# Local attention's transposes and weighted values two steps behind its scores

## The chip, the cores and the metric
The kernel runs on one NeuronCore of one Trainium2 chip. The metric is the device time of one execution in microseconds (us); the median of three runs stands for a kernel. Engines go by their short names: PE (TensorE), DVE (VectorE), ACT (ScalarE), POOL (GpSimd), SP (SyncE, which only issues DMAs).

## The reference
A decoder trunk of two layers over 1024 tokens of width 1024. Each layer normalizes x, projects it with one matrix `w_in`, and feeds three mixers side by side; their gated results go through `w_out` and are added to x.

```python
h = rms_norm(x, norm_g); proj = h @ w_in                # split into the parts below
y_mla  = mla_mixer(q_lat, kv_lat, k_rope, ...) * silu(g_mla)   # latent attention, causal
y_conv = short_conv_mixer(c_h, c_b, c_c, conv_w) * silu(g_conv)
y_swa  = swa_mixer(s_q, s_k, s_v, ...) * silu(g_swa)    # local attention, window 128
x = x + concat([y_mla, y_conv, y_swa]) @ w_out
```

The change is in `swa_mixer`: 8 query heads in two groups (`kv` 0 and 1) of four heads that share keys and values; queries and keys normalized per head; a block of 128 queries sees its own 128 keys and the 128 before; scores get a distance penalty, a softmax with one extra "sink" logit, and then weight the values.

## The kernel before
Products are made as three fp32r matmuls of high and low parts (`mm3`, lines 188 to 190). Each layer has three phases. **Phase 1** (pool `p1`) makes all local attention, and beside it the projections of the latents and a part of the gates. **Phase 2** (pool `cp`) makes the rest of the projection and the convolution; its `u` tiles are in a pool `uc` of their own on the right side of the memory. **Phase 3** makes the output projection and the latent attention.

Phase 1 is a software pipeline written out by hand. Its list `steps` has 17 entries: (kv 0, block 0 to 7), an empty one, (kv 1, block 0 to 7). A step goes through four functions:

- `swa_a` (a): projects 320 columns (24 matmuls), ACT squares, DVE sums, POOL takes the inverse root, DVE writes the normalized `qn` (line 316).
- `swa_b` (b): PE transposes `qn` (L326, L329), ACT and DVE write high and low parts of keys and queries `sx` (L333 to L337); PE makes the scores in `ps_s` (L350, 8 matmuls); DVE adds the penalty and takes maxima (L354, four, each followed by a short read of its maximum); ACT takes exponentials into a tile `pr` (L359) and DVE the reciprocals of the sums; POOL scales `pr` (L365, four heads). `ps_s` has one buffer, `pr` two.
- `swa_d` (d): PE transposes the scaled `pr` (L375, 8), ACT and DVE write their high and low parts `sy` (L376, L377, two each).
- `swa_e` (e): PE multiplies by the values (L385, 4 matmuls), ACT moves half of it (L389, L390), DVE adds into `osw` (L393, two).

The order within one iteration i is `'badfe'`: b of step i-1, a of step i, d of step i-2, then `f`, then e of step i-2. `f` runs as many "units" as the list `P1_FILL` says for that iteration: eight `unit_b` and eight `unit_a` (latents and values, 24 matmuls of 256 or 288 columns), then gate units `unit_m` (24 matmuls of 512 columns, an ACT copy L410 and a store L412). When certain units are done, `fill` asks for the weights of later ones (`after`): four loads on SP (L149) into three raw tiles, casts (L171) and subtractions (L173). Gate weights 0 are asked for behind the sixteenth unit and gate weights 1 behind the twentieth; the units right behind these use them.

The program text gives priorities; the order of instructions on each engine is laid down when the kernel is built, by a planned time. On the chip each engine then takes its instructions in that order, and a waiting instruction holds what stands behind it.

Of the kernel before, what the change touches and what calls it, by code (L numbers as in the profile page):

```python
# [10 lines left out]
F32 = mybir.dt.float32  # L11
# [8 lines left out]
P = 128  # L20
# [26 lines left out]

X_BEFORE, X_ALONE, X_FREE = 1, 7, 2
P1_ORDER = 'badfe'
P1_FILL = ([0, 0, 2, 1, 0, 1, 1, 2, 1, 2, 0, 0, 2, 1, 0, 1, 0, 2, 0, 1],  # L50
           [2, 2, 2, 2, 0, 0, 2, 1, 1, 1, 1, 1, 0, 1, 1, 1, 1, 1, 1, 1])
C1_STEP = 3
O_STARTS = [0, 0, 0, 0, 0, 0, 0, 0, 0, 0, 0, 0, 0, 1, 0, 0, 0, 0, 2, 0, 2, 1, 2, 1, 1, 1, 3, 2, 0, 0, 0, 0]
O_LIGHT = [0, 0, 0, 0, 0, 0, 0, 0, 0, 0, 0, 0, 0, 0, 0, 0, 0, 0, 0, 0, 0, 0, 0, 0, 0, 0, 0, 0, 1, 1, 0, 2]
# [9 lines left out]
def f32(ap):  # L64
    return ap.bitcast(F32)
# [3 lines left out]
def trunk(ctx, tc, x, norm_g, w_in, w_qb, w_kvb, w_out, c_gain, c_rope, c_idb, c_ali, out):  # L69
# [4 lines left out]
    def phase_pool(name, bufs=1):  # L74
        cm = tc.tile_pool(name=name, bufs=bufs, reuse_waits="tile")
        return cm, cm.__enter__()
# [23 lines left out]
    def ps_s():  # L100
        return pp["pool"].tile([P, 1024], F32, name="ps_s", tag="S", bufs=pp["n"][0])

    def ps_t():
        return pp["pool"].tile([P, 512], F32, name="ps_t", tag="T", bufs=pp["n"][1])
# [140 lines left out]
    for l in range(depth):  # L245
# [45 lines left out]
        def load_c(kv):  # L291
            return load_w([win[:, :, O_SQ + kv * 256:O_SQ + kv * 256 + 256],
                           win[:, :, O_SK + kv * 64:O_SK + kv * 64 + 64]], 8, eng=(v, g) if kv == 1 else g)

        uc_cm = tc.tile_pool(name=f"uc{l}", bufs=2, reuse_waits="tile", side="right")
        uc = uc_cm.__enter__()
        p1_cm, p1 = phase_pool(f"p1{l}")
        ali = p1.tile([P, H, 2 * P], BF16, name="ali")
        if l:
# [8 lines left out]
        def swa_a(kv, t, w):  # L308
            o = group_mm(t, w, WMAX)
            qn = p1.tile([P, 5, 2, 64], F32, name="qn", tag="qn", bufs=2)  # L310
            sq = qn.rearrange("p h o d -> p (h o d)")[:, 0:WMAX]
            s.activation(out=sq, in_=o, func=AF.Square)
            ss = small.tile([P, 5], F32, name="sss")
            v.tensor_reduce(out=ss, in_=sq.rearrange("p (h d) -> p h d", h=5), axis=AX.X, op=ALU.add)
            r = rsqrt("sr", ss, 5, 1.0 / 64, EPS)
            v.tensor_tensor(
                out=qn,
                in0=o.rearrange("p (h o d) -> p h o d", h=5, o=1).broadcast_to([P, 5, 2, 64]),
                in1=r.rearrange("p (h o u) -> p h o u", o=1, u=1).broadcast_to([P, 5, 2, 64]),
                op=ALU.mult)  # L320
            wq[kv, t] = qn.rearrange("p h o d -> p (h o d)")

        def swa_b(kv, t):
            qf = wq.pop((kv, t))
            tk = ps_t()
            pe.transpose(tk[:, 0:P], qf[:, 4 * P:5 * P], idn)  # L326
            tq = ps_t()
            for h in range(4):
                pe.transpose(tq[:, h * P:(h + 1) * P], qf[:, h * P:(h + 1) * P], idn)  # L329
            qs = qst[:, t % 2]  # L330
            kh = kst[:, 0, (t + 1) * P:(t + 2) * P]
            kl = kst[:, 1, (t + 1) * P:(t + 2) * P]
            s.mul(kh, tk[:, 0:P], skg[:, l:l + 1])  # L333
            v.scalar_tensor_tensor(out=kl, in0=tk[:, 0:P], scalar=skg[:, l:l + 1],
                                   in1=f32(kh), op0=ALU.mult, op1=ALU.subtract)
            s.mul(qs, tq, sqg[:, l:l + 1])
            v.scalar_tensor_tensor(out=qs[64:128], in0=tq[64:128], scalar=sqg[64:128, l:l + 1],  # L337
                                   in1=f32(qs[64:128]), op0=ALU.mult, op1=ALU.subtract)
            sc = ps_s()
            m = small.tile([P, 4], F32, name="sm")  # L340
            nm = small.tile([P, 4], F32, name="snm")
            ls = small.tile([P, 4], F32, name="sls")
            es = small.tile([P, 4], F32, name="ses")
            ri = small.tile([P, 4], F32, name="sri")
            pr = p1.tile([P, 4, 256], F32, name="pr", tag="pr", bufs=2)
            k0 = 0 if t else P
            sk4 = snk[:, l, kv * 4:kv * 4 + 4]
            for h in range(4):
                for a in range(2):
                    pe.matmul(sc[:, h * 256:(h + 1) * 256], lhsT=qs[:, h * P:(h + 1) * P],  # L350
                              rhs=kst[:, a, t * P:(t + 2) * P], start=(a == 0), stop=(a == 1))
            for h in range(4):
                so = sc[:, h * 256:(h + 1) * 256]
                v.tensor_tensor_reduce(out=so[:, k0:], in0=so[:, k0:], in1=ali[:, kv * 4 + h, k0:], scale=1.0,  # L354
                                       scalar=sk4[:, h:h + 1], op0=ALU.add, op1=ALU.max, accum_out=m[:, h:h + 1])
            v.tensor_scalar(out=nm, in0=m, scalar1=-1.0, scalar2=None, op0=ALU.mult)
            v.tensor_tensor(out=es, in0=sk4, in1=m, op=ALU.subtract)
            for h in range(4):
                s.activation(out=pr[:, h, k0:], in_=sc[:, h * 256 + k0:(h + 1) * 256], func=AF.Exp,  # L359
                             bias=nm[:, h:h + 1], scale=1.0, accum_out=ls[:, h:h + 1])  # L360
            marks["exp"] = s.activation(out=es, in_=es, func=AF.Exp)
            v.tensor_tensor(out=ls, in0=ls, in1=es, op=ALU.add)
            v.reciprocal(out=ri, in_=ls)  # L363
            for h in range(4):
                g.tensor_scalar(out=pr[:, h, k0:], in0=pr[:, h, k0:], scalar1=ri[:, h:h + 1], scalar2=1.0,  # L365
                                op0=ALU.mult, op1=ALU.mult)
            wprob[kv, t] = pr

        def swa_d(kv, t):
            pr = wprob.pop((kv, t))  # L370
            blks = (0, 1) if t else (1,)
            for blk in blks:
                tp = ps_t()
                for h in range(4):
                    pe.transpose(tp[:, h * P:(h + 1) * P], pr[:, h, blk * P:(blk + 1) * P], idn)  # L375
                s.copy(out=pts[:, blk, 0], in_=tp)  # L376
                v.tensor_tensor(out=pts[:, blk, 1], in0=tp, in1=f32(pts[:, blk, 0]), op=ALU.subtract)  # L377
# [68 lines left out]
        steps = [(0, t) for t in range(NT)] + [None] + [(1, t) for t in range(NT)]  # L446

        def fetch(key, parts, **how):
            W[key] = load_w(parts, 8, **how)
# [13 lines left out]
        def fill(n=1):  # L463
            for _ in range(n):
                k = n_done[0]
                if k == len(units):
                    return
                if k >= 2 * NT and k % 4 == 0:
                    W["gate"] = W[k // 4 - NT // 2, "g"]
                units[k]()  # L470
                n_done[0] += 1
                if k in after:
                    key, parts = after[k]
                    if key == "a":
                        fetch(key, parts)
                    else:
                        fetch((key, "g"), parts, **({"eng": v, "cast": s.copy} if key > 1 else {}))
                if k == 2 * NT - 1:
                    nc.sync.dma_start(out=lat_d, in_=latf[:, :NT * 416])

        nf = P1_FILL[min(l, 1)]
        if l == 0:
# [2 lines left out]
                if k >= X_FREE:  # L485
                    fill(1)
        fill(nf[0])
        for i in range(len(steps) + 2):
            cur, prv, old = (steps[k] if 0 <= k < len(steps) else None for k in (i, i - 1, i - 2))
            for op in P1_ORDER:  # L490
                if op == "b" and prv:
                    swa_b(*prv)
                if op == "a" and cur:
                    swa_a(*cur, W[cur[0]])
                if op == "d" and old:
                    swa_d(*old)
                if op == "e" and old:
                    swa_e(*old)
                if op == "f":
                    if i == C1_STEP:  # L500
                        W[1] = load_c(1)
                    fill(nf[i + 1])
            if pending and i:
                pending.pop(0)()
        close(p1_cm)

        cp_cm, cp = phase_pool(f"cp{l}")

        def st():
# [707 lines left out]
```

## Time and profile before

| | us |
|---|---|
| median of three runs | 1569.14 |
| lowest and highest of them | 1568.62, 1573.13 |
| the profiled execution, its whole time | 1572.78 |
| its span, first to last instruction | 1571.0 |
| PE busy in the span | 1488.8 |

The profile is one execution. Each engine's instructions have a start and a duration; where an engine sat idle, the profile names what ended the idle time. The granted clock says at which share of full speed PE ran: 1.00 is 2.4 GHz and 0.50 is 1.2 GHz. Phase 1 of the first layer lies at about 50 to 246 us, that of the second at about 810 to 1026 us.

### The profile page before, as it was taken

The numbers are of one execution on the slowest core, as the hardware profiler recorded it, in microseconds if no ns is written. First come the engines' busy times: TensorE is split into PE (matmuls) and PEld (weight loads), VectorE is DVE, ScalarE is ACT, GpSimd is POOL, SyncE is SP. The second block draws the span as 40 slices with busy tenths as digits, with TensorE's granted clock in tenths as the row PEclk, the third lists the DMA queues.
The fourth block names the chain that finished last, engine by engine and source line by source line (L and its number), as shares of the span: only waits on it lengthen the run. The fifth ranks groups of instructions, "written<-read, shape, count | busy, mean of one in ns | idle before, by whom it ended". The sixth has DMA issues, their size and how long they took to land.

```text
span 1571.0 us, 25506 instructions
## 1 busy us (share of the span) xinstructions
PE 1488.8 (95%) x9084; PEld 1317.0 (84%) x9084; DVE 1104.3 (70%) x2197; ACT 721.6 (46%) x1755; POOL 737.6 (47%) x960
## 2 busy tenths in 40 slices
PE   6899989999999999999989898999999999999998
PEld 5898878788879988888788897778888899888887
DVE  6666676867685668887657755668677756788964
ACT  4354454423321258976524444443232212788851
POOL 6434431544435646874244433324444456568640
PEclk9999999999999999999999999999999999999999
DMA  6101221133356510013241102221332663100123
GB/s 206 34 1 29 85 74 54 34 94 94 101 185 183 182 48 1 8 56 107 81 130 34 29 1 85 74 55 45 103 94 87 210 209 124 48 1 15 48 75 134
DMA packets 119521, 127.98 MB, mean 81 GB/s; under 512 B 16737, under 2 KB 102625, under 8 KB 118626
## 3 DMA queue, kind: packets, MB, share of 16 engines
q1 hardware_dynamic: 119394, 126.35, 25.6%
q8 instruction: 72, 1.18, 0.3%
q14 instruction: 55, 0.45, 0.1%
HBM read 95.65 MB, written 30.67 MB: 80 GB/s over the span
## 4 chain that ended last, share of the span: by engine, by line
PE 75%; DVE 8%; ACT 7%; issue 4%; POOL 3%; DMA 2%; SPq 0%; POOLq 0%; ACTq 0%; DVEq 0%
PE ps_g L188 13%; PE ps_g L190 13%; PE ps_g L189 13%; PE ps_b L604 8%; PE ps_a L604 6%; PE ps_c L604 5%; PE ps_s L943 4%; PE ps_g L987 4%; DMA wraw<-in_w_in_dram 2%; PE ps_s L350 2%; ACT apr L956 2%; PE ps_g L385 2%; PE ps_t L973 1%; PE ps_t L375 1%; POOL wlo L173 1%
## 5 line engine op out<-in xcount | busy, mean ns | idle before, releaser
L173 POOL TENSOR_TENSOR wlo<-wraw,whi 128x512 fp32r<-128x512 f32 (+2 forms) x120 | 165.9, 1391 | 130.2 <-DVE whi L171 102.1
L188 PE MATMUL ps_g<-whi,xh 128*128 128x320 f32 (+2 forms) x512 | 158.6, 310 | 5.9 <-ACT pr L359 1.8
L190 PE MATMUL ps_g<-whi,xl 128*128 128x320 f32 (+2 forms) x512 | 156.9, 306 | 0.0
L189 PE MATMUL ps_g<-wlo,xh 128*128 128x320 f32 (+2 forms) x512 | 156.8, 306 | 0.0
L190 PE MATMUL ps_g<-whi,yl 128*128 128x256 f32 x512 | 148.1, 289 | 5.5 <-DVE yl L694 5.5
L188 PE MATMUL ps_g<-whi,yh 128*128 128x256 f32 x512 | 149.1, 291 | 0.5
L189 PE MATMUL ps_g<-wlo,yh 128*128 128x256 f32 x512 | 147.1, 287 | 0.0
L987 PE MATMUL ps_g<-pt,vs 128*128 128x256 f32 (+1 forms) x640 | 121.1, 301 | 13.7 <-DVE pt L982 8.5
L365 POOL TENSOR_SCALAR pr<-pr,sri 128x256 f32<-128x256 f32 (+1 forms) x128 | 59.2, 482 | 124.5 <-DVE sri L363 90.5
L987 PEld LDWEIGHTS ps_g<-pt,vs 128*128 128x128 f32 x640 | 91.9, 191 | 25.2 <-DVE pt L982 14.8
L982 DVE TENSOR_TENSOR pt<-ps_t,pt 128x512 fp32r<-128x512 f32 (+1 forms) x160 | 100.2, 632 | 17.3 <-ACT pt L981 15.0
L943 PE MATMUL ps_s<-kt,qh 96*128 96x512 f32 (+3 forms) x384 | 106.9, 363 | 1.0 <-ACT apr L956 0.3
L171 DVE CAST whi<-wraw 128x512 fp32r<-128x512 f32 (+2 forms) x128 | 79.6, 631 | 39.7 <-PE ps_b L604 15.9
L959 POOL TENSOR_SCALAR apr<-apr,ari 128x896 f32<-128x896 f32 (+2 forms) x80 | 72.0, 900 | 74.1 <-DVE ari L958 63.0
L190 PEld LDWEIGHTS ps_g<-whi,yl 128*128 128x128 f32 x512 | 100.3, 196 | 6.9 <-DVE yl L694 6.9
L188 PEld LDWEIGHTS ps_g<-whi,xh 128*128 128x128 f32 x512 | 99.8, 195 | 7.6 <-issue 2.8
L981 ACT CAST pt<-ps_t 128x512 fp32r<-128x512 f32 (+1 forms) x160 | 85.7, 543 | 36.1 <-PE ps_g L190 17.6
L947 DVE TENSOR_REDUCE am<-ps_s 128x1 f32<-128x128 f32 (+7 forms) x128 | 95.6, 750 | 9.3 <-PE ps_s L945 7.0
L188 PEld LDWEIGHTS ps_g<-whi,yh 128*128 128x128 f32 x512 | 100.5, 196 | 1.8 <-DVE xr L745 0.9
L189 PEld LDWEIGHTS ps_g<-wlo,xh 128*128 128x128 f32 x512 | 99.7, 195 | 1.4
L188 PE MATMUL ps_g<-xh,whi 128*128 128x512 f32 x256 | 100.7, 393 | 0.0
L189 PE MATMUL ps_g<-xl,whi 128*128 128x512 f32 x256 | 100.5, 393 | 0.0
(252 smaller groups left out, 4487.6 us busy)
## 6 DMA issues: line engine op xcount, KB each, us to landing
wraw<-in_w_in_dram SPq DMA_DIRECT2D x104, 256.0 KB, 2.9
wraw<-in_w_out_dram SPq DMA_DIRECT2D x80, 256.0 KB, 3.0
x1p<-xr SPq DMA_DIRECT2D x16, 512.0 KB, 3.3
p<-x1p SPq DMA_DIRECT2D x16, 512.0 KB, 3.6
x<-in_x_dram SPq DMA_DIRECT2D x8, 512.0 KB, 4.9
gm_d<-st SPq DMA_DIRECT2D x16, 256.0 KB, 2.0
a<-in_w_in_dram SPq DMA_DIRECT2D x16, 256.0 KB, 3.3
xr<-in_x_dram SPq DMA_DIRECT2D x8, 512.0 KB, 5.3
```

What stands on the lines that cost most here:

```text
L171: cast(out=hi, in_=raw)
L173: e.tensor_tensor(out=lo, in0=raw, in1=f32(hi), op=ALU.subtract)
L188: pe.matmul(o, lhsT=lh, rhs=rh, start=(i == 0), stop=False)
L189: pe.matmul(o, lhsT=lh, rhs=rl, start=False, stop=False)
L190: r = pe.matmul(o, lhsT=ll, rhs=rh, start=False, stop=(i == n - 1))
L604: pe.matmul(o, lhsT=a[:, k], rhs=b[:, k], start=(first and k == 0 and i == 0), stop=(k == 3 and i == 2), skip_group_check=True)
L943: pe.matmul(sp[:, kk], lhsT=a[:, hs], rhs=kt[0:QK, b, h, kk], start=(ai == 0), stop=(ai == 2 and c0 + w < n))
L947: v.tensor_reduce(out=m, in_=sp[:, :n], axis=AX.X, op=ALU.max)
L959: g.tensor_scalar(out=pr[:, :n], in0=pr[:, :n], scalar1=ri, scalar2=1.0, op0=ALU.mult, op1=ALU.mult)
L981: s.copy(out=pt[:, 0, lo_c:], in_=tp[:, lo_c:])
L982: v.tensor_tensor(out=pt[:, 1, lo_c:], in0=tp[:, lo_c:], in1=f32(pt[:, 0, lo_c:]), op=ALU.subtract)
L987: pe.matmul(av[:, q0:], lhsT=vb, rhs=pt[:, a, q * 256 + q0:(q + 1) * 256], start=(bb == 0 and bi == 0 and a == 0), stop=(last and bi == 1 ...
```

## The change
Functions d and e take step i-3 where they took step i-2, so the loop runs 20 iterations, not 19. A third buffer holds the one more `pr` that is alive. The pool `uc` is opened behind phase 1 instead of ahead of it. The units are spread anew: each layer still runs as many of them inside phase 1.

```diff
-P1_FILL = ([0, 0, 2, 1, 0, 1, 1, 2, 1, 2, 0, 0, 2, 1, 0, 1, 0, 2, 0, 1],
-           [2, 2, 2, 2, 0, 0, 2, 1, 1, 1, 1, 1, 0, 1, 1, 1, 1, 1, 1, 1])
+P1_FILL = ([0, 0, 2, 1, 0, 1, 1, 2, 1, 1, 1, 0, 1, 1, 1, 1, 0, 1, 0, 1, 1],
+           [2, 2, 2, 2, 0, 0, 2, 1, 1, 1, 1, 0, 1, 0, 1, 1, 1, 1, 1, 1, 1])
-        uc_cm = tc.tile_pool(name=f"uc{l}", bufs=2, reuse_waits="tile", side="right")
-        uc = uc_cm.__enter__()
         p1_cm, p1 = phase_pool(f"p1{l}")
-            pr = p1.tile([P, 4, 256], F32, name="pr", tag="pr", bufs=2)
+            pr = p1.tile([P, 4, 256], F32, name="pr", tag="pr", bufs=3)
-        for i in range(len(steps) + 2):
-            cur, prv, old = (steps[k] if 0 <= k < len(steps) else None for k in (i, i - 1, i - 2))
+        for i in range(len(steps) + 3):
+            cur, prv, old = (steps[k] if 0 <= k < len(steps) else None for k in (i, i - 1, i - 3))
-                    fill(nf[i + 1])
+                    fill(nf[i + 1] if i + 1 < len(nf) else 0)
         close(p1_cm)
+        uc_cm = tc.tile_pool(name=f"uc{l}", bufs=2, reuse_waits="tile", side="right")
+        uc = uc_cm.__enter__()
         cp_cm, cp = phase_pool(f"cp{l}")
```

The first entry of each list runs ahead of the loop; entry i+1 belongs to iteration i.

## Rows read from the trace of the kernel before
**Rows 1.** The page's busy times: engine, busy us, share, instructions.
```profile
PE 1488.8 (95%) x9084; PEld 1317.0 (84%) x9084; DVE 1104.3 (70%) x2197; ACT 721.6 (46%) x1755; POOL 737.6 (47%) x960
```
**Rows 2.** Windows: stretch, length, busy us per engine, PE clock, DMA; phase 1 twice.
```profile
50.00:246.00 196.00, 178.54 (x1132) 162.33 (x1131) 129.87 (x352) 90.96 (x293) 78.94 (x130) 0.97 0.15 46
810.00:1026.00 216.00, 200.24 (x1289) 183.26 (x1288) 137.78 (x364) 95.77 (x311) 87.19 (x144) 0.96 0.15 45
```
**Rows 3.** PE's waits, 40 to 260 us: us in total, times, longest.
```profile
PE ps_t L375 <- POOL pr L365: 6.6, 3, 3.8
PE ps_g L385 <- ACT sy L376: 3.5, 7, 0.6
PE ps_s L350 <- DVE sx L337: 3.4, 1, 3.4
PE ps_s L350 <- ACT pr L359: 2.4, 1, 2.4
```
**Rows 4.** PE's waits, 800 to 1040 us.
```profile
PE ps_g L385 <- ACT sy L376: 4.7, 6, 1.6
PE ps_t L375 <- POOL pr L365: 2.3, 2, 1.9
PE ps_s L350 <- DVE sx L337: 2.2, 4, 1.0
...
PE ps_s L350 <- ACT pr L359: 1.8, 1, 1.8
```
**Rows 5.** PE in order of time, first layer's end: start, us, instruction, idle before it.
```profile
205.03 0.44 PE L375 MATMUL ps_t<-idn,pr 128*128 128x128 f32 x2 [1.70 <-POOL pr L365]
...
213.14 0.39 PE L189 MATMUL ps_g<-xl,whi 128*128 128x512 f32 x1
213.37 0.39 PE L190 MATMUL ps_g<-xh,wlo 128*128 128x512 f32 x1
...
219.06 1.20 PE L350 MATMUL ps_s<-sx 128*128 128x256 f32 x8
...
231.28 2.06 PE L375 MATMUL ps_t<-idn,pr 128*128 128x128 f32 x8 [3.82 <-POOL pr L365]
233.29 2.07 PE L350 MATMUL ps_s<-sx 128*128 128x256 f32 x8
```
**Rows 6.** Windows of 5 us where PE's clock fell, both layers.
```profile
230.00:235.00 5.00, 3.73 (x16) 2.87 (x17) 3.38 (x8) 3.40 (x9) 1.85 (x4) 0.60 0.14 52
235.00:240.00 5.00, 5.00 (x18) 4.05 (x18) 2.56 (x11) 1.98 (x9) 0.00 (x0) 0.72 0.01 3
895.00:900.00 5.00, 2.20 (x11) 1.91 (x12) 3.89 (x13) 1.35 (x7) 4.41 (x7) 0.66 0.25 59
900.00:905.00 5.00, 4.28 (x19) 3.77 (x18) 3.32 (x10) 3.93 (x14) 3.03 (x7) 0.50 0.12 41
905.00:910.00 5.00, 5.00 (x33) 4.79 (x33) 0.74 (x3) 0.82 (x3) 0.02 (x1) 0.82 0.01 3
```
**Rows 7.** DVE in order of time, from 223 us.
```profile
223.09 0.69 DVE L173 TENSOR_TENSOR wlo<-wraw,whi 128x512 fp32r<-128x512 f32 x1 [1.41 <-ACT whi L171]
...
224.70 0.49 DVE L354 CUSTOM_DVE_ANT_0 ps_s<-ps_s,ali,gains 128x256 f32<-128x256 f32 x1
...
232.49 0.75 DVE L337 SCALAR_TENSOR_TENSOR sx<-ps_t,gains,sx 64x512 fp32r<-64x512 f32 x1
```
**Rows 8.** ACT and POOL in the same stretch.
```profile
228.13 0.47 ACT L359 ACTIVATE pr<-ps_s,snm 128x256 f32<-128x256 f32 x1 [3.10 <-DVE ses L357]
...
230.74 1.85 POOL L365 TENSOR_SCALAR pr<-pr,sri 128x256 f32<-128x256 f32 x4 [9.92 <-ACT gt L410]
```
**Rows 9.** PE's scores of two neighbouring steps, each beside one unit.
```profile
88.78 1.11 PE L350 MATMUL ps_s<-sx 128*128 128x256 f32 x8
...
99.48 1.20 PE L350 MATMUL ps_s<-sx 128*128 128x256 f32 x8
```
**Rows 10.** Waits of SP's queue, 200 to 270 us.
```profile
SPq L412 <- ACT gt L410: 15.2, 2, 12.6
```

## The prediction
> **What bounds the kernel now.** I read the page's busy times first: PE is busy for 1488.8 of 1571.0 us and nobody else is near it [rows 1]. So an edit that adds and removes no instruction, as this one, can only win PE's idle time and the time in which PE ran at the lower clock. The windows come second, to see how much of both lies where the edit acts. In phase 1 PE is idle for 196.0 - 178.5 = 17.5 us of the first layer and 216.0 - 200.2 = 15.8 us of the second, and the mean clock is 0.97 and 0.96 [rows 2]; elsewhere in the span the edit touches nothing. Third, PE's waits in these two stretches say who ends the idle time. Four causes carry most of it: the transposes wait for the scaled probabilities from POOL (6.6 + 2.3 us), the weighted values wait for the eviction of those transposes (3.5 + 4.7 us), the scores wait for the keys and queries (3.4 + 2.2 us), and the scores wait for the exponentials of the step before, which hold the one score tile (2.4 + 1.8 us) [rows 3, 4]. The edit speaks to the first directly, to the second in part, to the other two not at all.
>
> Fourth, one such wait in order of time. At 227.5 us PE has run dry; the transposes start at 231.28 behind 3.82 us of idle time, the scores of the following step only at 233.29 [rows 5]. The reason lies up the chain: DVE stands in front of a weight subtraction that came late (1.41 us for ACT's cast), so the penalty of these scores starts at 224.70, though they were begun at 219.06 [rows 5, 7]; ACT's exponentials then start at 228.13 and POOL scales from 230.74 [rows 8]. After this gap the clock is at 0.60 and 0.72 in the next two windows [rows 6]: PE works at 1.2 GHz for a while.
>
> **The change, part by part.**
>
> *Transposes and values one iteration later.* Each of 16 steps per layer keeps its 8 (first block of a group: 4) transposes, its ACT casts, DVE subtractions, 4 (or 2) value matmuls, copies and adds; they move behind one more projection, one more score step and one more unit group. POOL's scaling (1.85 us for four heads, rows 8) isn't moved, so nothing on POOL's queue changes place. On ACT and DVE the moved evictions now stand beside the exponentials of a step two younger; per iteration their number is the same. What they give: the tile that the transposes read was scaled a whole iteration ago, so their wait goes: 6.6 + 2.3 = 8.9 us [rows 3, 4].
>
> *The clock.* In the first layer the lower clock after 231 us lasts 2 x (0.40 x 5 + 0.28 x 5) = 6.8 us, nearly all of it busy; work done at half speed there costs 3.3 us more than at full speed [rows 6]. It follows the longest of the removed waits, so I count it: 3.3. In the second layer the windows from 895 give 2 x (0.34 + 0.50 + 0.18) x 5 = 10.2 us at half speed, of which about 8.3 busy, a cost of 4.1 [rows 6]. That fall has a wait of 1.8 us for the exponentials in front of it, which stays, beside one of 1.9 us for the probabilities, which goes [rows 4]. I count half: 2.0.
>
> *Values behind their eviction.* Where an iteration has no unit, nothing stands between transposes and values, and PE waits up to 0.6 us (first layer) or 1.6 us (second) [rows 3, 4]. The moved step doesn't help by itself. The new spread does: iterations without a unit fall from six to four in the first layer (from three to four in the second), and both loops now end with a unit in each of the last two iterations. I count 3.0 of the 8.2 us; the bounds are nothing and 8.2.
>
> *Units.* The first layer's three double entries behind the seventh iteration become single. Two of these doubles ran a unit straight behind the request for its own weights, as at 213 us, the jam described above. A 512-column unit is 24 matmuls 0.23 us apart (213.14, 213.37), 5.5 us [rows 5]. Their number in phase 1 is the same, so their matmuls cost nothing more; what each had covered is uncovered where it leaves. The stores of their results on SP move along: a store already holds SP's queue for up to 12.6 us until its copy is there [rows 10], and weight loads issued behind a store wait with it. Bound: nothing, if the next loads are wanted an iteration later, up to one subtraction's delay as above, 1.4 us [rows 7], per load, four loads: 5.6. I take nothing, since the loads now have an iteration in between, and leave 5.6 in the range.
>
> *Third tile, and `uc` later.* No instruction. The first write to a `u` tile may now have to wait for memory of phase 1; it comes behind two further units (11 us of PE), which hide it; without that cover the longest hold-up of a store bounds it, 12.6 us [rows 10]. *One more iteration* holds no added work, only the shifted one.
>
> *Given back.* What is late next are the scores. At 227.5 us PE would find older transposes and values ready: 1.0 us for the transposes (half of the 2.06 at the lower clock) and 0.9 for the values (4 matmuls of 512 columns at 0.23 us) [rows 5], but the scores behind them need keys that DVE writes from 232.49 for 0.75 us [rows 7]: of the gap 1.9 us are surely filled, the rest only if the leftover unit (5.5 us) stands ahead of the scores in the order laid down. At 205.03 the wait of 1.70 us [rows 5] is covered by such a filler in full. I give back half of the remaining 1.9 us and half of the clock's 3.3 us (2.6 together), and 2.6 more for the second layer, where the wait for the exponentials may grow by what the probabilities' wait loses. Sum: 8.9 + 3.3 + 2.0 + 3.0 - 5.2 = 12.0 us. The profiled execution took 1572.8 us, 3.7 above the median of the runs; 1572.8 - 12.0 = 1560.8 in its terms, 1569.1 - 12.0 = 1557.1 as a median.
>
> The Trainium skill's page "Perfetto Trace Analysis", section "Optimization Strategy", says that a gap which repeats on the engine that should be full can mean that memory for the next tile isn't there. It names SBUF and PSUM alike. By that rule the third `pr` tile would be the wrong memory if the score tile in PSUM is the one that runs out; that case is the first rival.
>
> **The rivals.**
>
> *The wait changes its name.* The scores have one tile, and the next step's scores need the exponentials of the last: 2.4 + 1.8 us now, and 3.4 + 2.2 us for the keys, which ACT and DVE write behind those exponentials [rows 3, 4]. If this loop sets the pace, PE does the old step earlier and then stands before the scores instead. Then the 8.9 us and the clock go back, and the 3.0 us of the values stay: 1569.1 - 3.0 = 1566. For it: at the jam the keys come 0.75 us before the scores start, right behind [rows 5, 7]. Against it: elsewhere two neighbouring score steps lie 10.7 us apart (88.78 to 99.48) without such a wait [rows 9].
>
> *Slower: one unit is too little cover.* With doubles split, an iteration offers PE a projection (24 matmuls of 320 columns; by the 0.23 us of 512 columns an estimated 3.4), its scores (1.2) and query transposes (5 of the size of which 8 take 1.0: 0.6), old transposes and values (1.9) and one unit (5.5): 12.6 us. At the jam one step's scores lie 14.2 us behind the last (219.06 to 233.29) [rows 5]. Where a step's own chain is longer than 12.6 us, each iteration loses the difference, 1.6 us. The weight loads make the chain long, four of them per phase touch two iterations each: 8 x 1.6 = 13 us for both layers together, and one more stretch at the lower clock, 3.3; less the 12 of the forecast: 1573.5. Against it: the 10.7 us of rows 9, where one unit beside the step sufficed.
>
> *It doesn't do what it says.* The order is laid down by planned time; if the plan puts the older transposes where it had the younger ones, behind the scores, PE reaches them as late as before and the waits stay: 1569.
>
> *All of it.* The units fill every gap at the ends, nothing is given back and the values' waits go as well: 8.9 + 3.3 + 2.0 + 8.2 = 22.4, 1547.
>
> **How the numbers follow.** Forecast 1557 (1551 to 1564), chance 0.48. All of it, 1547: 0.11. The wait changes its name, 1566: 0.19. It doesn't do what it says, 1569: 0.06. Slower, 1573.5: 0.16. A measurement of this kernel tells 0.3%, 4.7 us, from no change: below 1564.4 is faster, above 1573.8 slower. Faster holds the forecast, all of it and a part of the first rival, 0.04: 0.63. Slower holds somewhat more than half of the last case, 0.13, and a load delayed as bounded above (1569 + 5.6) with 0.02: 0.15. The rest, 0.22, is the same. The range leaves out the far half of "all of it" and the upper half of "slower": 1546 to 1574.
>
> **What would show it.** Right: PE's waits no longer have a row of the transposes on POOL's probabilities; the windows of phase 1 give some 12 us less, and PE's clock near the end of the first layer's phase 1 stays at 1.00. Wrong in the first way: rows of the scores on keys or exponentials grow by what the transposes' row lost. Wrong in the second way: DVE or ACT waits for weights in an iteration with one unit, and the clock falls where it didn't before. The forecast fails above all if the order on ACT and DVE, which I can't see for the new text, puts evictions of the old step ahead of the exponentials that the next scores wait for.

## The result, and the profile after

The changed kernel takes 1544.1 us (1543.1 to 1546.2), the kernel before in the same comparison 1570.5: a ratio of 0.983 (95% interval 0.981 to 0.985), 26 us. The forecast was a gain of 12 us, to 1557, with a range that ended at 1546: the measured time lies below it. The sign was right, the forecast size was less than half of the measured one.

In the profiled execution (1543.1 us) no engine has fewer instructions, yet PE is busy for 1472.6 us where it was 1488.8 [rows 1]:

```profile
PE 1472.6 (96%) x9084; PEld 1307.6 (85%) x9084; DVE 1098.3 (71%) x2197; ACT 719.0 (47%) x1755; POOL 732.0 (47%) x960
```

To compare equal work I take phase 1 of each layer with the start of phase 2, from the last transpose of x to the first product of phase 2; both kernels run the same matmuls there. Windows (stretch, length, busy us of PE, PEld, DVE, ACT and POOL, PE clock, DMA), first of the kernel before, then of the changed one:

```profile
60.90:301.00 240.10, 221.68 (x1282) 195.85 (x1280) 164.23 (x383) 109.69 (x312) 93.65 (x133) 0.97 0.16 48
836.30:1080.00 243.70, 227.94 (x1319) 201.66 (x1319) 165.36 (x384) 110.18 (x316) 93.15 (x133) 0.96 0.16 47
```
```profile
60.80:284.80 224.00, 214.91 (x1282) 191.79 (x1283) 161.05 (x381) 107.65 (x311) 90.83 (x132) 1.00 0.18 51
819.50:1050.20 230.70, 219.17 (x1318) 197.41 (x1317) 162.91 (x384) 108.92 (x315) 91.03 (x133) 0.99 0.17 49
```

These two stretches give 16.1 + 13.0 = 29.1 us, all that the two profiled executions differ by (29.7). PE's idle time falls by 9.3 + 4.2 = 13.6 us. Its busy time, for the same matmuls, falls by 6.8 + 8.8 = 15.5 us: that is the clock, which is now 1.00 and 0.99. So in this pair more than half of the gain is matmuls that run faster, not gaps that closed. (Summed over windows of 2 us, PE stood at 1.2 GHz for 13.7 + 17.0 = 30.7 us of these stretches before, and for 0 + 3.4 us after.) The profiled execution of before has one of that kernel's lower clocks: its mean over the span is 0.983, where the executions of before measured beside the experiments have 0.982 to 0.990, on average 0.986; those of the changed kernel have 0.992 to 0.994. By these averages I estimate the clock's part of the 26 us between the medians at some 11 us (0.014 x 1571 - 0.007 x 1541), less than half.

PE's waits after, first layer, then second (us in total, times, longest); code lines behind 296 have moved up by two, so L348 is L350 of before, L373 is L375, L383 is L385:

```profile
PE ps_g L383 <- ACT sy L374: 4.6, 5, 1.6
PE ps_g L188 <- ACT xh L215: 1.1, 1, 1.1
PE ps_g L383 <- DVE sy L375: 1.0, 2, 0.6
PE ps_t L324 <- DVE qn L314: 0.9, 1, 0.9
...
PE ps_t L373 <- POOL pr L363: 0.2, 1, 0.2
```
```profile
PE ps_s L348 <- ACT pr L357: 3.2, 2, 1.9
PE ps_t L373 <- DVE sx L332: 2.7, 2, 1.4
PE ps_g L383 <- ACT sy L374: 2.6, 3, 1.1
PE ps_t L324 <- DVE qn L314: 2.6, 2, 1.7
```

The transposes' wait for POOL is down from 8.9 us [rows 3, 4] to 0.2. In the first layer the scores no longer have a row; it was 5.8 us [rows 3]. In the second they wait for exponentials a little longer, 3.2 us against 1.8 [rows 4], but a projection that also waited 1.8 us for exponentials no longer does, and two waits are new or nearly so: the transposes of `qn` for the normalized rows, and the old transposes for a PSUM tile that DVE holds while it writes keys (0.2 us before).

### The profile page after: what moved, and what is told of

It reads as the page before. It is cut to its first block, busy times and chain, and to the rows that moved or that the text cites. A ratio compares the mean times of both kernels' runs of the same rounds, so it can differ in the third digit from the quotient of the medians.

```text
span 1541.2 us, 25529 instructions
## 1 busy us (share of the span) xinstructions
PE 1472.6 (96%) x9084; PEld 1307.6 (85%) x9084; DVE 1098.3 (71%) x2197; ACT 719.0 (47%) x1755; POOL 732.0 (47%) x960
## 4 chain that ended last, share of the span: by engine, by line
PE 77%; DVE 8%; ACT 7%; issue 3%; POOL 3%; DMA 2%; SPq 0%; POOLq 0%; DVEq 0%; ACTq 0%
PE ps_g L188 13%; PE ps_g L190 13%; PE ps_g L189 13%; PE ps_b L604 8%; PE ps_c L604 6%; PE ps_a L604 6%; PE ps_s L943 4%; PE ps_g L987 4%; ACT apr L956 2%; PE ps_t L973 1%; PE ps_g L383 1%; PE ps_s L348 1%; DVE pt L982 1%; DMA wraw<-in_w_in_dram 1%; ACT pt L981 1%
## 5 line engine op out<-in xcount | busy, mean ns | idle before, releaser
L171 DVE CAST whi<-wraw 128x512 fp32r<-128x512 f32 (+2 forms) x128 | 75.8, 605 | 40.0 <-DMA wraw<-in_w_out_dram 16.2
L189 PEld LDWEIGHTS ps_g<-wlo,yh 128*128 128x128 f32 x512 | 100.3, 196 | 0.1
L190 PE MATMUL ps_g<-xh,wlo 128*128 128x512 f32 x256 | 100.0, 391 | 0.0
```

Source lines behind the costliest of these rows:

```text
L171: cast(out=hi, in_=raw)
L189: pe.matmul(o, lhsT=lh, rhs=rl, start=False, stop=False)
L190: r = pe.matmul(o, lhsT=ll, rhs=rh, start=False, stop=(i == n - 1))
```

## The experiments

| kernel | median us | ratio to before (95%) | phase 1, both layers | PE idle in it | at 1.2 GHz |
|---|---|---|---|---|---|
| before | 1570.5 | | 483.8 | 34.2 | 30.7 |
| changed | 1544.1 | 0.983 (0.981 to 0.985) | 454.7 | 20.6 | 3.4 |
| e1 lag, old spread | 1550.7 | 0.987 (0.985 to 0.988) | 462.8 | 23.2 | 13.6 |
| e2 new spread, lag 1 | 1570.8 | 1.000 (0.999 to 1.001) | 482.5 | 33.4 | 30.7 |
| e3 tile and pool alone | 1572.4 | 1.000 (1.000 to 1.001) | 485.2 | 34.0 | 34.1 |
| e4 before, scaled twice | 1594.6 | 1.015 (1.013 to 1.017) | 507.6 | 46.7 | 47.8 |
| e5 changed, scaled twice | 1556.5 | 0.991 (0.989 to 0.992) | 468.0 | 26.4 | 13.7 |
| e6 lag in 2nd group only | 1559.8 | 0.993 (0.991 to 0.995) | 471.2 | 28.5 | 20.5 |
| e7 lag in 1st group only | 1559.0 | 0.992 (0.991 to 0.994) | 471.3 | 27.6 | 20.5 |
| e8 first step alone late | 1573.6 | 1.001 (1.000 to 1.002) | 484.4 | 36.5 | 20.4 |
| e9 before, gaps filled | 1570.9 | 1.000 (0.998 to 1.001) | 480.7 | 28.0 | 17.1 |
| e10 mixed spread | 1543.8 | 0.982 (0.980 to 0.983) | 457.6 | 19.7 | 10.2 |
| e11 lag of three | 1539.9 | 0.980 (0.978 to 0.981) | 452.6 | 18.5 | 10.2 |
| e12 lag of three, scaled twice | 1549.3 | 0.986 (0.984 to 0.988) | 464.5 | 25.3 | 23.9 |

The last three columns come from one profiled execution each (phase 1 with the start of phase 2 as above; the last column is 2 x (1 - clock) x length, summed over windows of 2 us). The median of before moved between 1570.4 and 1571.9 from comparison to comparison. The profiled execution of e12 lies 4 us above its median, so its last three columns are on the high side.

**Which part of the change does it.** e1 takes the changed kernel and spreads the units as before:

```diff
-P1_FILL = (...,1, 1, 1, 0, 1, 1, 1, 1, 0, 1, 0, 1, 1],
-           [2, 2, 2, 2, 0, 0, 2, 1, 1, 1, 1, 0, 1, 0, 1, 1, 1, 1, 1, 1, 1])
+P1_FILL = (...,1, 2, 0, 0, 2, 1, 0, 1, 0, 2, 0, 1, 0],
+           [2, 2, 2, 2, 0, 0, 2, 1, 1, 1, 1, 1, 0, 1, 1, 1, 1, 1, 1, 1, 0])
```

> The lag of two steps, the third tile and the later pool, with the units spread as before (a zero is added for the twentieth iteration). Theory 1 (the lag takes the transposes' wait away, and with the short gaps go the stretches at the lower clock): most of the 26 us, 1545 to 1551, and at most two of the four stretches at the lower clock in phase 1 are left. Theory 2 (the spread does it: units no longer run straight behind the request for their own weights): at most 10 us, 1560 or more, with the first layer's stretch at about 230 us still there. Theory 3 (any new order laid down at the build would have moved the time): no forecast of size, but then the next kernels move too.

e2 takes the kernel before with the new spread (`..., 1, 0, 1, 0, 2]` and `..., 1, 1, 1, 2]` at the ends).

> The units' new spread alone, lag of one step, two tiles; the last two entries of each list are joined, since the loop has 19 iterations. Theory 1: within 5 us of the kernel before, 1565 to 1575; the transposes still wait for POOL, some 9 us in all. Theory 2: 1552 to 1560, and the first layer's late stretch at the lower clock is gone. Theory 3: any time between 1545 and 1575.

e3 takes the kernel before with `bufs=3` for `pr` and the pool `uc` opened behind phase 1.

> The third tile of probabilities and the later pool alone; lag and spread as before. Theories 1 and 2: the time of before within 2 us, since the second tile was free in time. Theory 3, or a wait for a free tile that the profile does not name: several us either way.

The lag alone gives 20.6 of the 26 us; the spread alone gives nothing (1.000). On top of the lag the spread is worth another 6.6 us by the medians, though the two intervals just touch. e3 has the same order of instructions on every engine as the kernel before, and the same time: the memory costs and gives nothing. By the times theory 1 holds, theory 2 falls, and theory 3 finds no support: e2 has a new order on every engine and the old time.

The waits say more than the times. In e1 the first layer's late stretch at the lower clock, theory 2's sign, is still there, and the transposes wait for POOL in front of it, though their step is two behind:

```profile
235.98 2.05 PE L373 MATMUL ps_t<-idn,pr 128*128 128x128 f32 x8 [2.77 <-POOL pr L363]
```
```profile
235.00:240.00 5.00, 3.50 (x12) 2.33 (x13) 2.35 (x6) 1.68 (x4) 1.84 (x4) 0.53 0.00 0
```

e1 keeps the old table's double at this end, which runs a unit straight behind the request for its weights. With the new table under the lag this wait and this stretch are gone, and the first layer's phase 1 takes 224.0 us, not 234.7; the second layer takes 2.6 us more. Whether it is this one double or the rest of the table was not tested by itself. In e2, without the lag, the transposes' wait for POOL is 1.3 + 2.2 = 3.5 us, not the 9 that theory 1 expected, and yet no time is gained: the scores wait 5.7 + 3.2 = 8.9 us for exponentials, where it was 4.2 [rows 3, 4]. There the wait only changed its name.

The Trainium skill ("Perfetto Trace Analysis", section "Optimization Strategy") reads repeating gaps as a possible lack of SBUF or PSUM for the next tile; here one more SBUF tile by itself moved nothing, 1.000. A second score tile in PSUM was not tried.

**How much slack.** e4 and e5 double POOL's scaling in the kernel before and in the changed one:

```diff
+            for h in range(4):
+                g.tensor_scalar(out=pr[:, h, k0:], in0=pr[:, h, k0:], scalar1=1.0, scalar2=1.0, ...)
```

> The kernel before with POOL's scaling of the probabilities done twice (the second time by 1): each step's chain to its transposes is 1.9 us longer, POOL has 60 us more work of its 830 idle. Theory 1: the transposes wait longer wherever they waited, 23 places: 15 to 40 us slower, 1585 to 1610, with more time at the lower clock. Theory 2: this chain does not set the pace, 0 to 6 us slower.

> The changed kernel with POOL's scaling done twice. Theory 1 (slack of a whole iteration): the added 1.9 us per step vanish in the slack, 1544 to 1550. Theory 2 (slack of the chain is not what counts): as much slower as the kernel before became with the same edit.

Before, it costs 23 us; after, 12. Half of it vanishes where my theory said nearly all of it, and the wait that I had in mind carries neither cost. In e4 the transposes wait 3.5 + 3.0 = 6.5 us for POOL, less than the 8.9 of before; what grew is the wait of the values for their casts (8.2 to 14.0 us), that for the normalized rows (none to 9.0) and the time at 1.2 GHz (30.7 to 47.8). In e5 the transposes wait 0.5 us for POOL in the first layer and not at all in the second. So that the lag halves the cost is measured; that it does so by slack between scaling and transposes is not shown. e11 and e12 ask whether one more step of lag takes the rest away (`pr` with four tiles, old step i-4, one iteration more, without a unit):

> The changed kernel with a lag of three steps and a fourth tile (one more iteration, without a unit). Theory 1 (one iteration of slack is more than the chain needs): no further gain, 1543 to 1549, a little slower for the longer end of the loop. Rival (slack is still short, as the 12 us that the doubled scaling cost the changed kernel may say): 1538 to 1542.

> Lag of three steps, four tiles, and POOL's scaling done twice. The doubled scaling cost the kernel of before 23 us and the changed kernel 12. Theory 1 (what it costs is the missing slack between scaling and transposes): with one more step of slack it costs under 5 us, 1540 to 1545. Rival (the second scaling holds POOL's queue, and what stands behind it there, the inverse roots of the next projection, comes late whatever the lag): it costs 9 to 14 us again, 1549 to 1554, with PE's waits for the normalized rows.

The lag of three has the lowest median of the study, 1539.9 us, as its rival said, 4 below the changed one with intervals that just touch; the gain is in the first layer, where phase 1 takes 219.8 us against 224.0:

```profile
60.60:280.40 219.80, 212.96 (x1284) 191.61 (x1284) 160.36 (x381) 107.47 (x311) 92.31 (x132) 1.00 0.18 52
816.50:1049.30 232.80, 221.09 (x1319) 199.38 (x1317) 168.68 (x384) 109.56 (x317) 91.34 (x134) 0.98 0.17 49
```

The doubled scaling costs it 9.4 us again, a size on the rival's side. PE's waits in e12, first layer's first and second layer's first rows (behind the added lines L386 and L377 are L385 and L376 of before):

```profile
PE ps_g L386 <- ACT sy L377: 6.2, 3, 3.8
PE ps_t L324 <- DVE qn L314: 2.8, 2, 2.6
```
```profile
PE ps_t L324 <- DVE qn L314: 6.0, 2, 4.3
PE ps_g L386 <- ACT sy L377: 3.7, 3, 2.6
```

No row of the transposes on POOL is left, and the rows for the normalized rows, which POOL's inverse roots feed, are there as the rival said. But the lag of three without doubling has them just as long (2.2 + 6.4 = 8.6 us against 8.8), so they can't be what the doubling costs. What grew is the values' wait for ACT's casts, from 1.9 + 1.5 to 6.2 + 3.7 us, and the time at 1.2 GHz, from 10.2 to 23.9. The longest of these waits, 3.77 us at 216.9, ends with a cast that stood on ACT behind the cast of a weight tile, which itself waited for its load:

```profile
214.05 0.62 ACT L171 CAST whi<-wraw 128x512 fp32r<-128x512 f32 x1 [1.54 <-DMA wraw<-in_w_in_dram]
...
216.31 0.59 ACT L377 CAST sy<-ps_t 128x512 fp32r<-128x512 f32 x1
```

How the doubled scaling brings this about stays open.

**Where the lag works.** e6 gives the lag of two steps to the second group of heads only, e7 to the first only:

```diff
+            prev = steps[i - 2] if 0 <= i - 2 < len(steps) else None
+            old = old if old and old[0] == 1 else prev if prev and not (prev[0] == 1) else None
```

> The changed kernel, but the lag is two steps only for the second group of heads (steps behind the empty one); the first group follows by one step as before. Spread and tiles as changed. Theory 1: the first half of each phase 1 loses its gain: the stretch at the lower clock at about 72 to 82 us comes back, and of the 26 us some 10 go: 1552 to 1558. Theory 2 (the spread, which differs only in the second half): 1544 to 1547.

> The changed kernel, but the lag is two steps only for the first group of heads; the second follows by one step as before. Theory 1: the gain of the first half stays, that of the second goes but for the spread's part: 1554 to 1562, and with the kernel above the two losses add up to about 26 us. Theory 2: 1550 or less, since the spread stays.

Each half carries about half: 15.7 and 14.9 us are lost (e6 is 2 us beyond its forecast range), 30.6 together against 26.4, so they add up but for a few us. And the early stretch at the lower clock, of which my prediction doesn't speak, belongs to the lag. Windows from 70 to 80 us of the kernel before, of the changed one, and of e6, in which only the first group goes back:

```profile
70.00:75.00 5.00, 1.56 (x11) 1.30 (x10) 4.35 (x10) 2.93 (x11) 3.44 (x6) 0.90 0.53 131
75.00:80.00 5.00, 4.54 (x19) 4.04 (x20) 3.63 (x13) 1.34 (x3) 2.44 (x5) 0.50 0.22 60
```
```profile
70.00:75.00 5.00, 4.48 (x32) 4.00 (x30) 4.73 (x14) 3.78 (x14) 4.83 (x5) 1.00 0.61 146
75.00:80.00 5.00, 5.00 (x41) 4.96 (x40) 3.88 (x11) 2.15 (x5) 3.55 (x7) 1.00 0.44 110
```
```profile
70.00:75.00 5.00, 1.56 (x10) 1.30 (x9) 4.35 (x10) 2.93 (x11) 3.44 (x7) 0.83 0.56 129
75.00:80.00 5.00, 4.54 (x19) 4.04 (x19) 3.63 (x13) 1.34 (x3) 2.32 (x5) 0.50 0.20 59
```

Here PE waited 3.4 us for keys and queries [rows 3], not for probabilities. ACT in order of time shows what the lag has to do with it; the kernel before:

```profile
67.54 0.37 ACT L389 COPY otmp<-ps_g 64x256 f32<-64x256 f32 x1
67.92 0.37 ACT L390 COPY otmp<-ps_g 64x256 f32<-64x256 f32 x1
68.31 0.37 ACT L333 ACTIVATE sx<-ps_t,gains 128x128 fp32r<-128x128 f32 x1
70.62 0.47 ACT L359 ACTIVATE pr<-ps_s,snm 128x256 f32<-128x256 f32 x1 [1.95 <-DVE snm L356]
...
72.53 0.70 ACT L336 ACTIVATE sx<-ps_t,gains 128x512 fp32r<-128x512 f32 x1
```

and the changed kernel:

```profile
69.82 0.36 ACT L331 ACTIVATE sx<-ps_t,gains 128x128 fp32r<-128x128 f32 x1
70.07 0.69 ACT L334 ACTIVATE sx<-ps_t,gains 128x512 fp32r<-128x512 f32 x1
70.64 0.59 ACT L374 CAST sy<-ps_t 128x512 fp32r<-128x512 f32 x1
71.50 0.47 ACT L357 ACTIVATE pr<-ps_s,snm 128x256 f32<-128x256 f32 x1 [0.27 <-DVE snm L354]
```

Before, the copies of the old step's values stood in front, and the queries' eviction (L336) came behind the exponentials, which waited for DVE: the next scores had to wait for both. After, the queries are evicted ahead of the exponentials (L334 before L357). e8 moves that one step alone, in the kernel before:

```diff
+            if i == 2:
+                old = None
...
+                if op == "d" and i == 3:
+                    swa_d(*steps[0])
+                    swa_e(*steps[0])
```

> The kernel before, lag of one step and old spread, with one step moved: the first step's transposes and values wait one iteration more and run just ahead of the second step's (third tile and later pool as in the change). Theory 4 (the old step's evictions stood on ACT and DVE in front of the eviction of the next keys, so that those fell behind the exponentials; that made the gap of 3.4 us at 74 us, which no transposes' wait explains): the gap and the lower clock at 72 to 82 us are gone, 4 to 7 us faster, 1564 to 1568, and nothing else of the gain is there. Rival (the gap is the weight load's: four casts on DVE in the same place): gap and lower clock stay, 1569 to 1573.

In its first layer the scores' wait for keys and queries is 0.2 us, down from 3.4, and ACT's order at 70 us is that of the changed kernel (L331, L334, L374, then L357): the old step's place was the cause of that gap, and the rival falls. The rest of theory 4 falls too, since nothing is gained. PE of e8 in order of time, and its windows, in the same place:

```profile
71.12 0.50 PE L383 MATMUL ps_g<-sy 128*128 128x512 f32 x1 [0.85 <-ACT sy L374]
72.93 0.50 PE L383 MATMUL ps_g<-sy 128*128 128x512 f32 x1 [1.31 <-DVE sy L375]
...
75.65 0.69 PE L373 MATMUL ps_t<-idn,pr 128*128 128x128 f32 x2 [1.12 <-POOL pr L363]
```
```profile
70.00:75.00 5.00, 2.38 (x13) 1.42 (x11) 4.72 (x14) 4.10 (x15) 4.84 (x5) 1.00 0.66 157
75.00:80.00 5.00, 4.35 (x22) 3.90 (x23) 3.48 (x14) 2.71 (x11) 1.96 (x5) 0.66 0.41 98
```

The gap of 3.4 us gave way to three of 3.3 us together: the moved step's values wait for their evictions, and the second step, which has no lag, for POOL. The clock falls all the same. Over the first layer the transposes' wait for POOL is 8.0 us (6.6 before), and in the second the values wait 8.2 us. Taking one gap away gained nothing here.

**What the clock does.** e9 puts work into PE's queue that nobody needs, ahead of three gaps of the kernel before:

```diff
+        def filler():
+            o = ps_t()
+            xh = xT[0][0]
+            for _ in range(9):
+                pe.matmul(o, lhsT=xh[:, 0, 0:P], rhs=xh[:, 0, 0:512], start=True, stop=True)
```

> The kernel before with nine matmuls of 512 columns, whose result nobody reads, put into PE's queue ahead of each of three of its gaps (first layer at about 68 and 227 us, second layer at about 893 us): 2.0 us of added work each. Theory 1, its part on the clock (gaps of this length make the clock fall, and the fall costs as much as the gap): the gaps shrink by the added work, the stretches at the lower clock behind them are shorter or gone, and the time is the same or up to 8 us less, 1562 to 1571, although PE does 6 us more. Rival (the clock falls for another reason, or its fall costs nothing since PE waits there anyway): the stretches stay, 1571 to 1578. The order laid down changes in other places too, so the stretches themselves count more than the total.

The calls stand ahead of the scores of block 2 of the first group (first layer), of the transposes of block 6 of the second group (first layer) and of the scores of block 6 of the first group (second layer). PE in order of time, first layer: the two fillers, and the gaps that are left behind them (3.44 and 3.82 us before; L358, L343 and L385 are L350, L337 and L375 of before).

```profile
67.44 2.33 PE L327 MATMUL ps_t<-xh 128*128 128x512 f32 x9
...
74.65 1.22 PE L358 MATMUL ps_s<-sx 128*128 128x256 f32 x8 [1.37 <-DVE sx L343]
...
226.50 2.25 PE L327 MATMUL ps_t<-xh 128*128 128x512 f32 x9
...
229.37 1.40 PE L385 MATMUL ps_t<-idn,pr 128*128 128x128 f32 x6 [0.62 <-DVE sx L340]
```

The clock stays at 1.00 behind both:

```profile
75.00:80.00 5.00, 4.43 (x34) 4.15 (x32) 4.57 (x14) 1.68 (x4) 2.29 (x4) 1.00 0.19 57
230.00:235.00 5.00, 4.27 (x25) 3.62 (x26) 4.20 (x14) 1.26 (x3) 0.51 (x2) 1.00 0.04 14
```

The first layer's phase 1 takes 235.8 us against 240.1, though PE does 4.6 us more: with the gaps filled, the falls of the clock behind them are gone, and they had cost real time. (A fall of 3.4 us elsewhere in that layer, at about 165 us behind a gap of 1.9, is new.) In the second layer the filler landed too early, at 885 us, a stretch at about 900 us stayed (6.8 us, 10.2 before), and that layer took 1.2 us more. Over the whole kernel the median is unchanged (1.000), but the mean granted clock of e9's ten executions is 0.988 to 0.992, on average 0.990, against 0.983 to 0.989, on average 0.985, in the nineteen of before beside it. By these averages I estimate that about 7 us of cost at the lower clock are gone (0.0146 x 1570 - 0.0101 x 1569), and the three fillers put 6.9 us of work in their place.

What no single profile shows is how far such a fall repeats. e3 runs the same instructions in the same order as the kernel before, so its profile is a second execution of that order. The same wait of the scores for exponentials, with the window around it, in the kernel before:

```profile
167.63 1.22 PE L350 MATMUL ps_s<-sx 128*128 128x256 f32 x8 [2.37 <-ACT pr L359]
```
```profile
165.00:170.00 5.00, 2.63 (x20) 2.35 (x19) 3.71 (x13) 3.15 (x12) 1.76 (x4) 1.00 0.84 342
```

and in e3:

```profile
167.34 2.07 PE L348 MATMUL ps_s<-sx 128*128 128x256 f32 x8 [2.36 <-ACT pr L357]
```
```profile
165.00:170.00 5.00, 2.66 (x11) 2.57 (x12) 2.89 (x10) 2.85 (x11) 1.84 (x4) 0.70 0.75 302
```

Behind the same gap the clock stayed at 1.00 once and fell once. The fall at about 74 us came in both, for 6.8 us and for 3.4. So differences of a few us in the last column of the table are within what one order gives from execution to execution; e9's clocks over ten executions and the 27 us between before and after are not.

**The spread again.** e10 is the changed kernel with the new spread in the first layer and the old one in the second, which had been faster there (228.1 in e1 against 230.7).

> The changed kernel with the new spread in the first layer only and the old one in the second, where phase 1 with the old spread took 228.1 us and with the new one 230.7. If layers are independent: 2 to 3 us less than the changed kernel, 1541 to 1543. If not: 1544 to 1547.

The second layer took 232.0 us, not 228.1. Its order on every engine differs in places from that of e1's second layer, though the table is the same, so what is laid down there depends on the first layer; some 1.7 us of the difference are the clock (6.8 us at 1.2 GHz against 3.4). Its first layer has the changed kernel's order and took 225.6 us against 224.0, again with 3.4 us more at 1.2 GHz. The median, 1543.8, is that of the changed kernel: the hoped-for 2 to 3 us did not come.

## Why the prediction was wrong, and what it had right

The forecast put 8.3 us on idle time (8.9 + 3.0 - 3.6) and 3.7 on the clock (3.3 + 2.0 - 1.6). The two profiled executions have 13.6 and 15.5.

*The clock* is the term that failed by its size: 3.7 us counted, 15.5 us of PE's busy time measured (some 11 by the estimate over all executions). Two of the four stretches in phase 1 (at about 72 and 950 us) I left out, because no long wait of the transposes lay in front of them. The one at 950 comes with five short waits of 0.3 to 0.6 us and a longer one that my list of causes doesn't have:

```profile
952.46 0.61 PE L188 MATMUL ps_g<-whi,xh 128*128 128x320 f32 x1 [1.82 <-ACT pr L359]
```

Yet the mean clocks stood in [rows 2]: 2 x (0.03 x 196 + 0.04 x 216) = 29 us at 1.2 GHz, some 15 us of cost, and I named these numbers without turning them into a bound. Of the stretch at about 900 us I counted half, since a wait of 1.8 us would stay; all of it went.

*"The edit speaks ... to the other two not at all"* is the step that failed in kind. The scores' waits for keys, queries and exponentials fell from 9.8 us [rows 3, 4] to 3.2. I had looked at the moved evictions as a constant number per iteration and didn't ask in front of whom they stood. The lag alone (e1) brings them to 2.8. e6 and the rows of ACT show how, for the gap at 74 us; e8 shows that gap's cause by itself. For the other waits of the scores, through which queue the lag acts is not shown.

*The transposes' wait*: 8.9 us counted, 8.7 gone. But the reason that I gave, a tile scaled a whole iteration ago, isn't enough: in e1 the lag alone leaves 3.1 us of it, 2.8 of them in one place, and e2 takes 5.4 us of it away without the lag and without a gain. That the sum came out so near is in part luck.

*Units*: nothing counted, and a bound for a loss alone. The jam behind a request for weights, which I had described, was still there under the lag (e1), and the new table took it away: 6.6 us by the medians on top of the lag, nothing without it (e2).

*Given back*, 5.2 us, 3.6 of them waits: more came than that, in other places. In the second layer the scores' wait for exponentials grew by 1.4 us and the two new rows hold 5.3; in the first layer the transposes of `qn` wait 1.4, some 8 us in all. The old waits that went, counted and not counted, were still more.

*Values behind their eviction*: 3.0 counted, 1.0 gone (9.8 with DVE's rows to 8.8), and against the reason given: in the first layer, where fewer iterations lack a unit, the wait grew from 4.1 to 6.2 us; in the second, where one more lacks it, it fell from 5.7 to 2.6. *Third tile and pool*: nothing counted, nothing measured (e3).

A reading to set right: the row at 232.49 us, which I took for the keys, is the low part of the queries (L337); the argument of the first rival stays the same.

Of the rivals, "the wait changes its name" is seen in small in the second layer, and in full with the spread alone (e2); "it doesn't do what it says" falls with the transposes' row; "one unit is too little cover" is refuted, since the first layer's phase 1 with single units is the shorter of the two spreads under the lag (224.0 against 234.7). "All of it" came nearest, and was still too small by the clock.

Idle time plus half of the time at 1.2 GHz, both as differences to the kernel before, account for phase 1's length within about 3 us in ten of the thirteen other kernels (with e9's fillers counted as work); e8 misses by 3.4, e11 by 5.2, e12 by 6.9. For the change they give -13.6 - 13.7 = -27.3 us against -29.1.

## What to carry to other kernels

In a software pipeline on engines that take their work in order, ask not only whether a late stage's input is ready, but which younger work its evictions stand in front of: one more step of lag alone also took away 7 of 9.8 us of waits for keys, queries and exponentials. Price a gap on TensorE with the clock: read the mean clock of the stage first, turn it into microseconds, and count it as the bound of what closing gaps can give back. And try a table of fill work together with the lag: the same table was worth 6.6 us with it and nothing without it. A shorter row of waits is no gain by itself; e2 lost 5.4 us of one row and grew another.

## What the runs showed of the hardware

In the profiled pair 13.6 us less idle time on PE came with 15.5 us less busy time for the same matmuls. One pair gives no rate: e11's profile has 2 us less idle time than the changed kernel's and 6.8 us more at 1.2 GHz. Useless matmuls in two gaps of 3.4 and 3.8 us kept the clock at 2.4 GHz behind them and shortened the stage, 240.1 to 235.8 us. The length of a single gap didn't settle it: behind the same gap of 2.4 us, in the same order of instructions, the clock stayed at 1.00 in one execution and fell in another, and the only fall left in the changed kernel's two stretches, at about 836 us, stands behind two gaps of 1.3 and 1.1 us:

```profile
833.71 1.21 PE L348 MATMUL ps_s<-sx 128*128 128x256 f32 x8 [1.27 <-ACT pr L357]
...
836.04 0.79 PE L383 MATMUL ps_g<-sy 128*128 128x512 f32 x1 [1.11 <-ACT sy L374]
```
```profile
835.00:840.00 5.00, 3.96 (x16) 3.87 (x17) 4.59 (x15) 1.59 (x6) 3.22 (x6) 0.66 0.28 66
```
